# Matmul operands at multiples of 512 bytes: small tiles move out from between the pools

## The chip, the cores and the metric

One core of a Trainium2 chip. The metric is the device time of the program in microseconds, the median of several runs. "PE" is TensorE, "PEld" its weight loads, "DVE" VectorE, "ACT" ScalarE, "POOL" GpSimd, "SP" the queue that issues all DMAs here. A matmul has a stationary operand, loaded ahead of it, and a moving operand that streams through it; in `mm<-al,ch` the moving one is `al`, the stationary one `ch`, and the result goes to `mm`.

## The reference

A two-layer decoder trunk on one sequence of 1024 tokens and 1024 channels, in float32:

```python
for l in range(DEPTH):                      # two layers
    hn = rms_norm(h, norm_mix_pre[l])
    if l < N_A_LAYERS:                      # layer A: RG-LRU with a causal conv and a GELU gate
        proj = hn @ w_in_a[a]
        ...
        y = rg_lru(xr, ...) * jax.nn.gelu(gate)
    else:                                   # layer B: sliding-window attention with sinks
        proj = hn @ w_in_b[b]
        ...
        y = sliding_window_attention_with_sinks(q, shared_k, shared_v, sinks[b])
    m_out = memory_attention(mq, mk, mv)    # 4 heads over 256 memory rows
    mixed = jnp.concatenate([y, m_out], axis=-1) @ w_out[l]
    h = h + rms_norm(mixed, norm_mix_post[l])
    f = swiglu_ffn(rms_norm(h, norm_ffn_pre[l]), w_ffn_in[l], w_ffn_out[l])   # 1024 -> 2816 -> 1024
    h = h + rms_norm(f, norm_ffn_post[l])
    if l == N_A_LAYERS - 1:                 # keys and values of all B layers, made once
        kv = rms_norm(h, norm_kv) @ w_kv_shared
```

## The kernel before

Everything is held transposed: channels in partitions, tokens along them, in tiles of 128 x 512 (two halves of the sequence). Each float32 operand is split into a high part, cast to the matmul's reduced type (`ah`, `wh`, `th`, `ch`), and a low part, the difference (`al`, `wl`, `tl`, `cl`). A product is three matmuls, high weight with low data, high with high, low with high, added up in one PSUM tile. Nearly all matmuls are of this kind, with 128 x 128 weights and 512 columns: L163 to L165 in the mixers' projections, L699 to L701 in the FFN's gate and up products (`gated`, with `al`/`ah` or `tl`/`th` as the data and `ch`/`cl` as weights), L807 to L809 in the FFN's output products (`out_step`). Both FFN matrix products are written as seven half-size products each instead of eight. Casts of weights run on ACT (L94), the subtractions for the low parts on DVE (L95).

The program runs in phases: a (layer A's mixer), f0 (its FFN, with the turn to layer B at the end), b (layer B's mixer), f1 (its FFN). A scheduler sets the order of instructions; manual dependencies (`after`, `place`, `pin`) hold the products in a given order. `finish` in `mix_out` adds the residual at the start of a phase f: its loads (L109, here into `th`/`tl`) feed DVE's L630.

Where a tile lies in its partition comes from the pools. Five pools stand for the whole program: `consts` (`cp`), `act` (`ap`, `ah` and `al`), `acc` (`fp`), `stat` (`sp`) and one in DRAM. Each phase then opens its own pools behind them, in the order in which `phase` gets them, and `reuse_waits="tile"` lets a tile of the next phase wait for just the tiles that lay in its place. A pool's start is rounded up to 32 bytes and no further, so a small tile in one pool shifts the start of all that follow. With 16 KB reserved and some constants, `cst` (560 bytes) starts at 16512, `ident` (the identity for transposes) behind it at 17088; `halo`, `carry`, `nm`, `sm`, `es`, `xr` (515 columns) stand between or ahead of larger tiles.

Where the operands of the 9,207 matmuls start, in bytes above a multiple of 512 (from the built program's addresses; 7,516 matmuls have 512 columns, 1,064 have 256):

| operand | before | after |
|---|---|---|
| moving | 480: 4,680; 160: 3,444; 192: 483; 96, 224, 288 or 416: 600 | 0: 8,724; 128: 385; 192: 98 |
| stationary | 160: 7,550; 224: 676; 480: 460; 416: 416; others: 105 | 0: 9,130; others: 77 |

Before, 480 is `ah` and `al`, 160 are `th`, `tl`, `ch`, `cl`, `wh`, `wl`, 192 is `ident` (385) and `ones` (98). All those of 512 columns start at an odd multiple of 32 bytes. After, 128 is `ident`, 192 `ones`, and the 77 are columns of `rc` and `ident`.

Of the kernel before, what the change touches and what calls it, by code (L numbers as in the profile page):

```python
# [7 lines left out]
F32 = mybir.dt.float32  # L8
# [5 lines left out]
P = 128  # L14
# [7 lines left out]
NL = 6  # L22
# [28 lines left out]
class Trunk:  # L51
# [190 lines left out]
    def rcol(self, s, tag, w=H):  # L242
        nc = self.nc
        nb = w // P
        st = self.psum("oo")
        s = s if isinstance(s, list) else [s]
        cells = [(j, x) for x in s for j in range(nb)]
        self.marks.append([nc.tensor.matmul(st[:, j:j + 1], x[:, j * P:(j + 1) * P], self.ones,  # L248
                                            start=i == 0, stop=i == len(cells) - 1)
                           for i, (j, x) in enumerate(cells)])  # L250
        rc = self.tile(self.sp, 1, f"rc{tag}", (P, nb), F32)
        self.mean = nc.vector.tensor_scalar(rc, st[:, :nb], 1.0 / D, EPS, op0=ALU.mult, op1=ALU.add)
        self.pow = nc.gpsimd.tensor_tensor(rc, rc, self.mhalf[:, :nb], op=ALU.pow)
        return rc
# [19 lines left out]

    def constants(self):
        nc, cp = self.nc, self.cp
        self.cst = cp.tile([P, NC_COLS], F32, name="cst")
        with self.tc.high_priority(offset=2 * WEIGHT_LEAD):
            nc.sync.dma_start(self.cst, self.a["cst"])
        self.ident = cp.tile([P, P], F32, name="ident")  # L280
        make_identity(nc, self.ident)
        self.ones = cp.tile([P, 1], F32, name="ones")
        nc.gpsimd.memset(self.ones, 1.0)
        self.mhalf = cp.tile([P, 4], F32, name="mhalf")
        nc.gpsimd.memset(self.mhalf, -0.5)

    def lambda_const(self, prev):
        nc, cp = self.nc, self.cp
        lam = self.cst[:, C_LAM:C_LAM + NL]
        t = [cp.tile([P, NL], F32, name=f"lam{i}") for i in range(5)]  # L290
        e, d, s, s2, h = t
        nc.scalar.activation(e, lam, AF.Abs)
        self.table(e, e, AF.Exp, scale=-1.0)
        self.after(nc.vector.tensor_scalar(d, e, 2.0, None, op0=ALU.add), prev)
        nc.vector.reciprocal(d, d)
        nc.vector.tensor_tensor(s, e, d, op=ALU.mult)
        nc.vector.tensor_tensor(s2, s, s, op=ALU.mult)
        self.after(nc.vector.memset(h, 1.0 / 19.0), prev)
        for q in (17, 15, 13, 11, 9, 7, 5, 3, 1):
            nc.vector.tensor_tensor(h, h, s2, op=ALU.mult)  # L300
            nc.vector.tensor_scalar(h, h, 1.0 / q, None, op0=ALU.add)
        nc.vector.tensor_tensor(h, h, s, op=ALU.mult)
        self.after(nc.vector.tensor_scalar(d, lam, 0.0, None, op0=ALU.min), prev)
        self.cl = cp.tile([P, NL], F32, name="cl")
        self.cl2 = cp.tile([P, NL], F32, name="cl2")
        nc.vector.scalar_tensor_tensor(self.cl, h, -2.0, d, op0=ALU.mult, op1=ALU.add)
        nc.vector.tensor_scalar(self.cl2, self.cl, 16.0, None, op0=ALU.mult)
        nc.vector.tensor_scalar(self.cl, self.cl, 8.0, None, op0=ALU.mult)
# [336 lines left out]
    def quad(self, x):  # L645
        return x.rearrange("p (k c) -> p k c", k=4)
# [358 lines left out]
    def run(self):  # L1005
        a = self.a
        self.constants()
        self.h1 = self.dp.tile([D, T], F32, name="h1")
        self.kv1 = [self.dp.tile([P, H], F32, name=f"mkv1_{i}") for i in range(2)]
        common = dict(s=2, sq=1, rsn=2)  # L1010
        att = dict(qs=2, pb=4, ph=2, pl=2, nm=6, sm=6, es=6)
        mix_w = dict(wraw=2, wh=2, wl=2)
        quad = lambda i: {f"t{h}{i}{k}": 1 for h in "hl" for k in range(4)}
        ffn = ({"mm": 7, "oo": 1}, dict(ch=4, cl=4), dict(c1=2, c6=1, c7=1, hd=7, x=1),
               dict(wq=6, wp=4), quad(2), quad(3), quad(1))
        self.phase("a", {"gt": 2, "mm": 3, "ss": 1, "tt": 1, "oo": 1}, mix_w, {**common, "sp": 1}, dict(rest=1),
                   dict(xr=4, graw=1, gwh=2, gwl=2, xc=2, xh=1, xl=1, gr=2, gi=2, a2=2), att)
        spare = [("xr", (P, 3 + H)), ("gr",), ("gi",), ("a2",)]
        mix = self.mix_out(0, *self.layer_a(), a["xT"], (), spare)
        self.phase("f0", *ffn)  # L1020
        h0, fin = self.ffn(0, *mix, self.h1, False)
        self.phase("b", {"mm": 3, "ss": 2, "tt": 2, "oo": 1}, dict(wh=3, wl=3), common, dict(rest=1), dict(r=1, kf=1),
                   {**att, "qs": 4, "pb": 6})
        mix = self.layer_b(h0, fin)
        self.phase("f1", *ffn)
        self.ffn(1, *mix, a["out"], True)
        self.stack.close()
# [343 lines left out]
```

## Time and profile before

| what | us |
|---|---|
| median of 3 runs (lowest, highest) | 1978.69 (1977.61, 1980.29) |
| the profiled execution, first to last instruction | 1975.6 |
| PE busy | 1948.1 (99%) |
| DVE busy | 1398.9 (71%) |
| ACT busy | 1015.4 (51%) |
| POOL busy | 420.9 (21%) |

The profiled execution's own time is not listed apart from its span; the runs lie 2.0 to 4.7 us above that span. A matmul's duration in the trace (some 390 ns) overlaps the next ones', so its cost is the distance from its start to the next start. A row of stages gives the stretch, its length, then for each engine its busy time and number of instructions, the granted clock of PE, the mean busy share of the DMA engines and GB/s. A row of the timeline gives start, duration, engine, line, operation and tiles; a row of groups ends in the group's busy time, the mean duration of one in ns, and the idle time before them.

### The profile page before, as it was taken

The page shows a single profiled execution, that of the slowest core. Times are in us where ns is not written, and L with a number is a line of the kernel's source. Part 1 is how long each engine was busy: PE and PEld are TensorE (multiplying, and loading weights), DVE is VectorE, ACT ScalarE, POOL GpSimd, SP SyncE. Part 2 cuts the span into 40 slices and gives each one's busy share as a digit, 9 for nine tenths or more (in the row PEclk, how much of TensorE's full clock was granted, in tenths as well). Part 3 has the DMA queues.
Part 4 walks back from the last instruction along what each step waited for, and adds up shares of the span by engine and source line. Part 5 has one row for each costly group of instructions (what it writes and reads, how often), then busy time and mean ns, then how long its engine had stood idle before and what let it go on. Part 6 is the DMA issues. An engine that isn't in the chain of part 4 may idle for free.

```text
span 1975.6 us, 27850 instructions
## 1 busy us (share of the span) xinstructions
PE 1948.1 (99%) x9382; PEld 1625.9 (82%) x9382; DVE 1398.9 (71%) x2319; ACT 1015.4 (51%) x1939; POOL 420.9 (21%) x435
## 2 busy tenths in 40 slices
PE   9999999999999999999999999999999999999997
PEld 7887888788888888888788888887888888888887
DVE  8888977976766676455786898669656665754567
ACT  6677974534444444454554778454333333344551
POOL 0122200034453320000035454100223232300001
PEclk9999999999999999999999999999999999999999
DMA  5522536167768789775663423361634544586663
GB/s 184 170 85 81 162 124 226 60 231 248 246 233 278 253 283 325 234 230 176 200 213 139 126 100 111 114 251 38 207 134 165 168 146 150 200 300 192 217 193 128
DMA packets 184686, 361.71 MB, mean 183 GB/s; under 512 B 20448, under 2 KB 26336, under 8 KB 184544
## 3 DMA queue, kind: packets, MB, share of 16 engines
q1 hardware_dynamic: 184544, 359.95, 54.4%
q8 instruction: 73, 1.20, 0.2%
q14 instruction: 69, 0.57, 0.1%
HBM read 251.86 MB, written 105.91 MB: 181 GB/s over the span
## 4 chain that ended last, share of the span: by engine, by line
PE 89%; DVE 6%; issue 2%; ACT 2%; DMA 2%; POOL 0%; SPq 0%; POOLq 0%; DVEq 0%; ACTq 0%
PE mm L699 12%; PE mm L701 12%; PE mm L700 12%; PE mm L807 7%; PE mm L808 7%; PE mm L809 7%; PE mm L163 7%; PE mm L165 7%; PE mm L164 7%; PE oo L1186 1%; PE tt L1179 1%; PE mm L679 1%; PE mm L678 1%; PE mm L680 1%; PE oo L248 1%
## 5 line engine op out<-in xcount | busy, mean ns | idle before, releaser
L94 ACT CAST ch<-wq 128x512 fp32r<-128x512 f32 x311 | 193.1, 621 | 426.9 <-PE mm L700 219.6
L95 DVE TENSOR_TENSOR cl<-wq,ch 128x512 fp32r<-128x512 f32 x311 | 233.6, 752 | 190.2 <-ACT ch L94 114.8
L699 PE MATMUL mm<-al,ch 128*128 128x512 f32 x640 | 252.8, 395 | 2.8 <-ACT c L729 2.8
L701 PE MATMUL mm<-ah,cl 128*128 128x512 f32 x640 | 250.9, 392 | 0.0
L700 PE MATMUL mm<-ah,ch 128*128 128x512 f32 x640 | 250.1, 391 | 0.0
L163 PE MATMUL mm<-al,wh 128*128 128x512 f32 x552 | 219.0, 397 | 0.5 <-ACT wh L94 0.5
L165 PE MATMUL mm<-ah,wl 128*128 128x512 f32 x552 | 217.9, 395 | 0.8 <-DVE wl L95 0.7
L164 PE MATMUL mm<-ah,wh 128*128 128x512 f32 x552 | 217.7, 394 | 0.0
L807 PE MATMUL mm<-tl,ch 128*128 128x512 f32 x532 | 207.5, 390 | 0.6 <-ACT ah L909 0.3
L808 PE MATMUL mm<-th,ch 128*128 128x512 f32 x532 | 207.0, 389 | 0.0
L809 PE MATMUL mm<-th,cl 128*128 128x512 f32 x532 | 206.4, 389 | 0.0
L699 PE MATMUL mm<-tl,ch 128*128 128x512 f32 x480 | 189.1, 394 | 0.0
L701 PE MATMUL mm<-th,cl 128*128 128x512 f32 x480 | 188.5, 393 | 0.1
L700 PE MATMUL mm<-th,ch 128*128 128x512 f32 x480 | 187.4, 390 | 0.0
L710 DVE TENSOR_TENSOR c<-c,mm 128x512 f32<-128x512 f32 x120 | 82.3, 686 | 107.2 <-PE mm L701 106.9
L699 PEld LDWEIGHTS mm<-al,ch 128*128 128x128 f32 x640 | 120.2, 188 | 29.5 <-ACT c L729 3.7
L701 PEld LDWEIGHTS mm<-ah,cl 128*128 128x128 f32 x640 | 120.1, 188 | 28.2
L700 PEld LDWEIGHTS mm<-ah,ch 128*128 128x128 f32 x640 | 120.2, 188 | 26.3
L165 PEld LDWEIGHTS mm<-ah,wl 128*128 128x128 f32 x552 | 103.8, 188 | 24.0 <-DVE wl L95 1.9
L163 PEld LDWEIGHTS mm<-al,wh 128*128 128x128 f32 x552 | 103.8, 188 | 21.4 <-ACT wh L94 0.9
L164 PEld LDWEIGHTS mm<-ah,wh 128*128 128x128 f32 x552 | 104.0, 188 | 21.0
L719 POOL TENSOR_TENSOR x<-wq,wq 128x512 f32<-128x512 f32 x36 | 49.5, 1375 | 328.5 <-DMA wq<-in_wi_dram 278.6
(415 smaller groups left out, 4310.4 us busy)
## 6 DMA issues: line engine op xcount, KB each, us to landing
wq<-in_wi_dram SPq DMA_DIRECT2D x168, 256.0 KB, 4.7
xz<-hd SPq DMA_DIRECT2D x154, 256.0 KB, 4.2
th<-xz SPq DMA_DIRECT2D x154, 256.0 KB, 3.6
wp<-in_wf_dram SPq DMA_DIRECT2D x112, 256.0 KB, 4.2
wz<-wp SPq DMA_DIRECT2D x88, 256.0 KB, 2.3
wq<-wz SPq DMA_DIRECT2D x56, 256.0 KB, 3.5
wraw<-in_wa_dram SPq DMA_DIRECT2D x26, 512.0 KB, 3.5
wq<-in_wf_dram SPq DMA_DIRECT2D x42, 256.0 KB, 3.8
```

The costliest lines, as they stand in the source:

```text
L94: self.cast = self.nc.scalar.copy(hi, src)
L95: return (eng or self.nc.vector).tensor_tensor(lo, src, hi.bitcast(F32), op=ALU.subtract)
L163: self.mms += [nc.tensor.matmul(out, wh, al, start=i == 0, stop=False), nc.tensor.matmul(out, wh, ah, start=False, stop=False), nc.tensor. ...
L164: nc.tensor.matmul(out, wh, ah, start=False, stop=False),
L165: nc.tensor.matmul(out, wl, ah, start=False, stop=i == len(ks) - 1)]
L699: ins += [mm(out, wh, xl, start=start and k == 0, stop=False, skip_group_check=not start), mm(out, wh, xh, start=False, stop=False, skip_g ...
L700: mm(out, wh, xh, start=False, stop=False, skip_group_check=not start),
L701: mm(out, wl, xh, start=False, stop=k == 3, skip_group_check=not start)]
L710: add = lambda o, x, y: nc.vector.tensor_tensor(o, x, y, op=ALU.add)
L807: ins += [mm(ps[m], wh[:, m], xl[:, cs], start=start and p == 0, stop=False, skip_group_check=not start), mm(ps[m], wh[:, m], xh[:, cs], s ...
L808: mm(ps[m], wh[:, m], xh[:, cs], start=False, stop=False, skip_group_check=not start),
L809: mm(ps[m], wl[:, m], xh[:, cs], start=False, stop=p == NFB // 2 - 1, skip_group_check=not start)]
```

## The change

Tiles that no matmul reads, or that are small, move away from between the matmul operands. `ident` goes ahead of `cst`. The small columns `rc` go from the pool `stat` to the constants, which fill up to a multiple of 512. The temporaries `lam0` to `lam4`, `xr`, `halo`, `carry`, `nm`, `sm`, `es` and `nsink` go to a last pool of phase a or b.

```diff
-        rc = self.tile(self.sp, 1, f"rc{tag}", (P, nb), F32)
+        rc = self.tile(self.cp, 1, f"rc{tag}", (P, nb), F32)
...
+        self.ident = cp.tile([P, P], F32, name="ident")
         self.cst = cp.tile([P, NC_COLS], F32, name="cst")
...
-        self.ident = cp.tile([P, P], F32, name="ident")
         make_identity(nc, self.ident)
...
-        t = [cp.tile([P, NL], F32, name=f"lam{i}") for i in range(5)]
+        t = [self.t(f"lam{i}", (P, NL)) for i in range(5)]
...
-        att = dict(qs=2, pb=4, ph=2, pl=2, nm=6, sm=6, es=6)
+        att, small = dict(qs=2, pb=4, ph=2, pl=2), dict(nm=6, sm=6, es=6)
...
         self.phase("a", {"gt": 2, "mm": 3, "ss": 1, "tt": 1, "oo": 1}, mix_w, {**common, "sp": 1}, dict(rest=1),
-                   dict(xr=4, graw=1, gwh=2, gwl=2, xc=2, xh=1, xl=1, gr=2, gi=2, a2=2), att)
+                   dict(graw=1, gwh=2, gwl=2, xc=2, xh=1, xl=1, gr=2, gi=2, a2=2), att,
+                   {**small, "xr": 4, "halo": 1, "carry": 1, **{f"lam{i}": 1 for i in range(5)}})
...
-                   {**att, "qs": 4, "pb": 6})
+                   {**att, "qs": 4, "pb": 6}, {**small, "nsink": 1})
```

The orders of PE and POOL hold the same instructions in the same order. On the other engines rows differ at one place, the turn from phase a to f0. There SP issues, before the change, the last of the residual loads (`tl`) and then the loads of FFN weights (`wq`):

```order
L109 DMA tl_726_3541<-in_xT_dram 128x512
L109 DMA tl_727_3548<-in_xT_dram 128x512
L109 DMA tl_728_3555<-in_xT_dram 128x512
L109 DMA tl_729_3562<-in_xT_dram 128x512
L653 DMA wq_3396<-in_wi_dram 128x512
L653 DMA wq_3398<-in_wi_dram 128x512
L653 DMA wq_3623<-in_wi_dram 128x512
L653 DMA wq_3625<-in_wi_dram 128x512
```

and with the change:

```order
L109 DMA tl_731_3545<-in_xT_dram 128x512
L109 DMA tl_732_3552<-in_xT_dram 128x512
L653 DMA wq_3400<-in_wi_dram 128x512
L109 DMA tl_733_3559<-in_xT_dram 128x512
L653 DMA wq_3402<-in_wi_dram 128x512
L653 DMA wq_3627<-in_wi_dram 128x512
L653 DMA wq_3629<-in_wi_dram 128x512
L653 DMA wq_3631<-in_wi_dram 128x512
L109 DMA tl_734_3566<-in_xT_dram 128x512
```

The third and fourth `tl` moved behind one and four loads of weights; they now lie where phase a's `qs` tiles lay, and wait for PE's last reads of those. At the same place ACT casts, before,

```order
L94 CAST th32_701_3368<-wq_711_3396 128x512
L94 CAST th33_703_3370<-wq_712_3398 128x512
L94 CAST ah_657_3151<-acc_602_2859 128x512
L94 CAST ah_659_3156<-acc_612_2903 128x512
L223 ACTIVATE sq_679_3267<-acc_678_3265 128x512
```

and with the change:

```order
L94 CAST th32_706_3372<-wq_716_3400 128x512
L94 CAST ah_662_3154<-acc_607_2862 128x512
L94 CAST th33_708_3374<-wq_717_3402 128x512
L94 CAST ah_664_3159<-acc_617_2906 128x512
L223 ACTIVATE sq_684_3270<-acc_683_3268 128x512
```

One cast of an FFN weight (`th33`) and one of the second half's activations (`ah`) changed places; DVE's subtractions for `tl33` and `al` do the same.

## The prediction

> **What bounds the kernel now.** I read the page first (busy times, then the chain that ended last), then the granted clock, then the busy times by stage, and then single matmuls in the timeline.
>
> ```profile
> span 1975.6 us, 27850 instructions
> ...
> PE 1948.1 (99%) x9382; PEld 1625.9 (82%) x9382; DVE 1398.9 (71%) x2319; ACT 1015.4 (51%) x1939; POOL 420.9 (21%) x435
> ...
> PE 89%; DVE 6%; issue 2%; ACT 2%; DMA 2%; POOL 0%; SPq 0%; POOLq 0%; DVEq 0%; ACTq 0%
> ```
>
> TensorE is busy for 99% of the span and carries 89% of the chain. Its idle time is 1975.6 - 1948.1 = 27.5 us. The clock is no issue:
>
> ```profile
> core 0: 1975.6 us, clock 0.997
> ```
>
> The stages (layer a's mixer, FFN 0 with its end, the turn to layer b, layer b, FFN 1, the tail), with PE, PEld, DVE, ACT, POOL, clock and DMA share:
>
> ```profile
> 0.00:400.00 400.00, 391.50 (x1911) 325.92 (x1912) 327.92 (x524) 274.25 (x470) 52.01 (x91) 1.00 0.41 136
> 400.00:950.00 550.00, 549.66 (x2411) 450.73 (x2410) 361.99 (x523) 247.81 (x438) 135.08 (x96) 1.00 0.74 249
> 950.00:1000.00 50.00, 49.19 (x228) 40.47 (x227) 38.75 (x69) 25.15 (x48) 4.88 (x4) 1.00 0.51 172
> 1000.00:1330.00 330.00, 325.12 (x1914) 284.69 (x1913) 257.10 (x582) 207.10 (x527) 118.74 (x167) 0.99 0.44 152
> 1330.00:1950.00 620.00, 618.12 (x2806) 509.96 (x2805) 399.77 (x586) 259.57 (x454) 108.83 (x77) 1.00 0.53 174
> 1950.00:1975.60 25.60, 14.52 (x122) 14.16 (x121) 13.34 (x37) 1.51 (x4) 1.41 (x2) 0.83 0.38 129
> ```
>
> In the two FFN stages (1170 us) TensorE has no idle time worth the name, VectorE is busy 65% of the time and the DMA engines 53 to 74%. In the mixers VectorE is at 82% and 78%. So the time is the number of matmuls times their distance, and a change that moves no instruction acts through that distance or not at all. The durations of matmuls overlap; the distance is taken from start to start. A long run in layer a (moving operands `al`, `ah`) and one in FFN 0's output product (`tl`, `th`), first and last row of each:
>
> ```profile
> 318.05 0.39 PE L165 MATMUL mm<-ah,wl 128*128 128x512 f32 x1
> ...
> 326.29 0.39 PE L165 MATMUL mm<-ah,wl 128*128 128x512 f32 x1
> ```
>
> ```profile
> 840.20 0.39 PE L807 MATMUL mm<-tl,ch 128*128 128x512 f32 x1
> ...
> 859.92 0.39 PE L807 MATMUL mm<-tl,ch 128*128 128x512 f32 x1
> ```
>
> The first holds 36 distances: 8.24 / 36 = 228.9 ns. The second holds 87: 19.72 / 87 = 226.7 ns. Same instruction, width and clock, another distance. What differs is where the moving operand starts: 480 bytes above a multiple of 512 in the first, 160 in the second (the table of starts stands with the change; the trace holds no addresses). Groups by operand, mean duration of one:
>
> ```profile
> L699 PE MATMUL mm<-al,ch 128*128 128x512 f32 x640 | 252.8, 395 | 2.8 <-ACT c L729 2.8
> L701 PE MATMUL mm<-ah,cl 128*128 128x512 f32 x640 | 250.9, 392 | 0.0
> L700 PE MATMUL mm<-ah,ch 128*128 128x512 f32 x640 | 250.1, 391 | 0.0
> ...
> L807 PE MATMUL mm<-tl,ch 128*128 128x512 f32 x532 | 207.5, 390 | 0.6 <-ACT ah L909 0.3 <-DVE tl L95 0.3
> L808 PE MATMUL mm<-th,ch 128*128 128x512 f32 x532 | 207.0, 389 | 0.0
> L809 PE MATMUL mm<-th,cl 128*128 128x512 f32 x532 | 206.4, 389 | 0.0
> L699 PE MATMUL mm<-tl,ch 128*128 128x512 f32 x480 | 189.1, 394 | 0.0
> L701 PE MATMUL mm<-th,cl 128*128 128x512 f32 x480 | 188.5, 393 | 0.1
> L700 PE MATMUL mm<-th,ch 128*128 128x512 f32 x480 | 187.4, 390 | 0.0
> ```
>
> The output product's mean of 389.3 goes with 226.7 ns, so a duration less 162.6 is a distance: 230.1 for `al`/`ah` (392.7), 229.7 for `tl`/`th` in the gate products (392.3). Weighted over the 640, 532 and 480 triples that is 229, and I use 229.1 for the 7,516 matmuls of 512 columns. What could they be? Around 1128 us the clock was halved for a moment (0.50 in the first row), and 256 columns ran there:
>
> ```profile
> 1127.70:1128.60 0.90, 0.90 (x6) 0.90 (x6) 0.87 (x5) 0.40 (x2) 0.90 (x3) 0.50 0.11 27
> ```
>
> ```profile
> 1127.71 0.41 PE L1186 MATMUL oo<-pl,vv 128*128 128x256 f32 x1
> ...
> 1128.56 0.41 PE L1179 MATMUL tt<-ident,pb 128*128 128x128 f32 x1
> ```
>
> Four distances, 0.85 / 4 = 212.5 ns at half clock, thus 106 at the full one and 213 for 512 columns. The 226.7 is 17/16 of 213.3, the 229.1 is 7.4% over it. At full clock 256 columns show the same proportion, with both kinds of start (160, then 480):
>
> ```profile
> 82.45 0.28 PE L355 MATMUL mm<-wh,al 128*128 128x256 f32 x1
> ...
> 83.36 0.28 PE L357 MATMUL mm<-wl,ah 128*128 128x256 f32 x1
> ```
>
> ```profile
> 1930.07 0.28 PE L807 MATMUL mm<-al,th 128*128 128x256 f32 x1
> ...
> 1931.01 0.28 PE L809 MATMUL mm<-ah,tl 128*128 128x256 f32 x1
> ```
>
> Eight distances each: 113.8 and 117.5 ns against 106. So the stretch grows with the columns, is absent at half clock (moving data come too slowly for the full clock, not for the half) and depends on the start. The weight load beside it is not the cause: of four matmuls before a pause the last had none beside it, and 1.07 = 3 x 0.227 + 0.39, its usual duration:
>
> ```profile
> 944.53 1.07 PE L809 MATMUL mm<-th,cl 128*128 128x512 f32 x4
> ...
> 944.54 0.64 PEld L809 LDWEIGHTS mm<-th,cl 128*128 128x128 f32 x3
> ```
>
> **The change, part by part.** *Instructions.* None is added or removed; TensorE's and GpSimd's orders are equal, and of the others a few rows swap at the turn from layer a to FFN 0. There two residual loads (`tl`) now wait until TensorE has read the `qs` tiles that lie in their place, with a weight load queued behind each on SP.
>
> ```profile
> 313.90 2.31 SPq L109 DMA_DIRECT2D tl<-in_xT_dram  x4
> 318.10 7.67 SPq L653 DMA_DIRECT2D wq<-in_wi_dram  x8
> ...
> L165 PE MATMUL mm<-ah,qs x4: 388/388/388, 303.2 to 305.3; 128*128 128x512 f32 x4
> ...
> 344.84 2.73 DVE L630 SCALAR_TENSOR_TENSOR acc<-acc,cst,tl 128x512 f32<-128x512 f32 x4
> ```
>
> `qs` is read for the last time at 305.7 (305.3 and its 0.39), 8 us ahead of these loads; VectorE wants the data at 344.8. The `wq` loads went out until 325.8 because they wait for VectorE, not for SP. I cost this at 0, covered by some 19 us; were the cover gone, a late load of some 5 us would be the price, once. The swap of one cast on ACT and one subtraction on VectorE (0.6 and 0.7 us) is 0 as well.
>
> *Small tiles.* `rc` and the lambda tiles are the same instructions at another place: 0.
>
> *Operand starts, 512 columns.* From an odd multiple of 32 bytes, 9,130 of 9,207 stationary and 8,724 moving operands go to a multiple of 512. No row shows a 512-column matmul from such a start. Bounds: 213.3 ns from below (the half-clock rows), and from above 232.5, the slowest stretch of several, in which moving and stationary operands start alike (all at 160):
>
> ```profile
> 1701.92 0.40 PE L699 MATMUL mm<-tl,ch 128*128 128x512 f32 x1
> ...
> 1702.85 0.39 PE L700 MATMUL mm<-th,ch 128*128 128x512 f32 x1
> ```
>
> (four distances, 0.93 / 4). I take 216, near the lower end, because all that the rows show of the stretch (proportion, clock, start) fits a read that begins inside a piece of the memory's own grid and has to fetch one piece more for every sixteen; on the grid this piece is gone. That is an inference, not a row. Gain: 7,516 x (229.1 - 216) = 98 us. The Trainium skill, "TensorE: Matmul & The Clock Gate", section "Back-to-back issue gap", gives N / 2.4 + 2.5, that is 216 ns for 512 columns, measured with bf16; by it this term would be the same 98 us, and the trace, with 226.7 at best, does not reach it today.
>
> *256 columns.* 1,064 matmuls, between 113.8 and 117.5 now, say 117; to 109 by the same proportion: 8.5 us.
>
> *Given back.* VectorE does the same work in less time. In 0 to 400 us it would be busy 328 of some 379 us (87% instead of 82%), in 1000 to 1330 us 257 of 313. TensorE's idle time there is 8.5 and 4.9 us; I let it double and take 10 us for both with the loads' tighter deadlines (the DMA share of 0.74 becomes 0.78). At worst the mixers gain nothing and only the 1170 us of the FFNs do: 106 x 1170 / 1976 = 63.
>
> Sum: 98 + 8.5 - 10 = 96 us off the profiled span of 1975.6, to about 1879. The median of the runs, 1978.7, lies 3.1 over that span, so 1978.7 - 96 = 1883. Own range of this case: 1866 (213.3 ns, nothing given back: 119 + 8.5 less some 15 that VectorE takes) to 1916 (63 gained).
>
> **The rivals.** *Another steady state.* The offset matters, but what is left is the 17/16, and all stretches fall to the best one seen: 7,516 x (229.1 - 226.7) = 18 and 1,064 x (117 - 113.8) = 3.4 us, thus 1957 (1950 to 1972). For it: 226.7 holds through runs of 20 us and more and looks like a lock. Against it: it takes a supply that is too slow for the full clock from any start.
>
> *Nothing.* The contents of a read are contiguous, and a start at a multiple of 32 may be as good as any; then 1979, within 4 us. The differences between 226.7 and 229 would come from the order of the tiles and stay. Against it: within one run of one kind the distance is steady, and it turns with the tile's pool. The Trainium skill, "SBUF — State Buffer", section "Specifications (TRN2)", speaks for this rival: the memory has lines of 16 bytes. Both starts are multiples of 16, so 2,048 bytes touch 128 lines before and after, and by that rule the time stays; the same rule would have no room for the two distances above.
>
> *Slower.* With all operands on one offset the moving and the stationary stream always start on the same part of the memory. If they hinder each other there, every 512-column matmul goes like the stretch at 1702 us: 7,516 x (232.5 - 229.1) = 26 us, thus 2004. For it: that stretch has equal offsets. Against it: the output products have equal offsets too, at 226.7, the best there is. It decides from a mean distance of 229.7 on (229.1 + 4 us / 7,516).
>
> **How the numbers follow.** Forecast 0.52, another steady state 0.18, nothing 0.14, slower 0.14, the rest below 1866. Within 0.2% (4 us, about what runs of this kernel tell from no change): 0.14. Faster by more: 0.52 + 0.18 + 0.02, rounded to 0.71. Slower: 0.15. The range reaches from 1866 over the forecast, the steady state and no change to 1981 and leaves out the slower case; the likeliest case alone has 1866 to 1916.
>
> **What would show it.** Right: 694 matmuls of the output product, 157 us of FFN 0 now, take about 150; group means of L699 to L701 and L807 to L809 fall alike to about 378; `al` and `tl` groups no longer differ. Idle time of TensorE grows in the mixers alone, behind VectorE. Wrong: group means at 389 everywhere (the steady state), unchanged and still apart (nothing), at 395 or over (slower). A late `tl` load would stand as a wait of L630 near 340 us. The step that I trust least is 216.

## The result, and the profile after

| | median us (lowest to highest, runs) | span of the profiled run |
|---|---|---|
| before | 1978.34 (1977.61 to 1980.29, 4) | 1975.6 |
| after | 1966.66 (1965.88 to 1969.17, 4) | 1964.7 |

The ratio is 0.9946 (95% interval 0.9931 to 0.996): faster by 0.5%, some 12 us by the medians and 11 by the spans, of the 96 that were forecast. The page after (span, busy times, chain):

```profile
span 1964.7 us, 27857 instructions
...
PE 1935.3 (99%) x9382; PEld 1626.5 (83%) x9382; DVE 1397.8 (71%) x2319; ACT 1015.5 (52%) x1939; POOL 426.0 (22%) x435
...
PE 88%; DVE 6%; ACT 2%; issue 2%; DMA 1%; POOL 1%; SPq 0%; POOLq 0%; DVEq 0%; ACTq 0%
```

TensorE's busy time fell by 12.8 us (1948.1 to 1935.3) and its idle time rose by 1.9 (27.5 to 1964.7 - 1935.3 = 29.4): 10.9 us of span. The stages that were shown of before, with PE, PEld, DVE, ACT, POOL, clock, DMA share:

```profile
0.00:400.00 400.00, 390.24 (x1915) 326.14 (x1916) 327.73 (x524) 274.61 (x471) 55.09 (x91) 1.00 0.40 136
400.00:950.00 550.00, 549.01 (x2427) 453.74 (x2427) 366.33 (x531) 250.74 (x444) 134.80 (x95) 1.00 0.73 250
...
1330.00:1950.00 620.00, 618.00 (x2874) 517.04 (x2875) 402.57 (x599) 258.50 (x453) 110.98 (x78) 1.00 0.53 176
```

The stretch from 400 to 950 us, nearly all of 512 columns, holds more matmuls (2,427 for 2,411) in the same busy time: each costs less. The last stretch (2,874 for 2,806) can't be read that way, since the program runs ahead and 78 more of its matmuls have 256 columns (250 for 172), while those of 512 fell from 2,580 to 2,556. How much less one costs is read from start-to-start distances in the timeline, for the two stretches that stood at 228.9 and 232.5 ns (the second with its block at another time now):

```profile
316.52 0.39 PE L165 MATMUL mm<-ah,wl 128*128 128x512 f32 x1
...
324.68 0.39 PE L165 MATMUL mm<-ah,wl 128*128 128x512 f32 x1
...
1691.21 0.39 PE L699 MATMUL mm<-tl,ch 128*128 128x512 f32 x1
...
1692.12 0.39 PE L700 MATMUL mm<-th,ch 128*128 128x512 f32 x1
```

36 distances in 8.16 us are 226.7 ns, four in 0.91 are some 227. In the groups, the gate products (L699 to L701) have come down to the 389 to 390 ns that the output products (L807 to L809) had before, and those have not moved. The mixers' projections (L163 to L165) have come down less, from 397, 394 and 395 to 395, 393 and 393.

```profile
L699 PE MATMUL mm<-al,ch 128*128 128x512 f32 x640 | 249.6, 390 | 2.9 <-ACT c L729 2.9
L700 PE MATMUL mm<-ah,ch 128*128 128x512 f32 x640 | 249.2, 389 | 0.0
L701 PE MATMUL mm<-ah,cl 128*128 128x512 f32 x640 | 249.0, 389 | 0.0
L163 PE MATMUL mm<-al,wh 128*128 128x512 f32 x552 | 218.2, 395 | 0.6 <-ACT wh L94 0.6
...
L807 PE MATMUL mm<-tl,ch 128*128 128x512 f32 x532 | 207.4, 390 | 0.6 <-ACT ah L909 0.3 <-DVE tl L95 0.3
L808 PE MATMUL mm<-th,ch 128*128 128x512 f32 x532 | 207.0, 389 | 0.0
L809 PE MATMUL mm<-th,cl 128*128 128x512 f32 x532 | 206.4, 389 | 0.0
L699 PE MATMUL mm<-tl,ch 128*128 128x512 f32 x480 | 187.4, 390 | 0.2
```

From the start times of all 512-column matmuls, leaving out distances over 250 ns (pauses), the mean went from 229.12 to 227.17 ns: 7,516 x 1.95 = 14.7 us. The matmuls of 256 columns became slower, from 117.2 to 119.4 ns (distances over 150 ns left out): 1,064 x 2.2 = 2.3 us the other way. 14.7 - 2.3 = 12.4 accounts for the 12.8 us of busy time.

### The profile page after: what moved, and what is told of

Read it like the earlier page. It is cut to its first block, busy times and chain, and to the rows that moved or that the text cites. A ratio compares the mean times of both kernels' runs of the same rounds, so it can differ in the third digit from the quotient of the medians.

```text
span 1964.7 us, 27857 instructions
## 1 busy us (share of the span) xinstructions
PE 1935.3 (99%) x9382; PEld 1626.5 (83%) x9382; DVE 1397.8 (71%) x2319; ACT 1015.5 (52%) x1939; POOL 426.0 (22%) x435
## 4 chain that ended last, share of the span: by engine, by line
PE 88%; DVE 6%; ACT 2%; issue 2%; DMA 1%; POOL 1%; SPq 0%; POOLq 0%; DVEq 0%; ACTq 0%
PE mm L699 12%; PE mm L701 12%; PE mm L700 12%; PE mm L807 7%; PE mm L808 7%; PE mm L809 7%; PE mm L165 6%; PE mm L163 6%; PE mm L164 6%; PE oo L1187 1%; PE tt L1180 1%; PE oo L248 1%; PE mm L679 1%; PE mm L678 1%; PE mm L680 1%
## 5 line engine op out<-in xcount | busy, mean ns | idle before, releaser
L699 PE MATMUL mm<-al,ch 128*128 128x512 f32 x640 | 249.6, 390 | 2.9 <-ACT c L729 2.9
L701 PE MATMUL mm<-ah,cl 128*128 128x512 f32 x640 | 249.0, 389 | 0.0
L163 PE MATMUL mm<-al,wh 128*128 128x512 f32 x552 | 218.2, 395 | 0.6 <-ACT wh L94 0.6
L165 PE MATMUL mm<-ah,wl 128*128 128x512 f32 x552 | 216.9, 393 | 0.9 <-DVE wl L95 0.9
L807 PE MATMUL mm<-tl,ch 128*128 128x512 f32 x532 | 207.4, 390 | 0.6 <-ACT ah L909 0.3
L808 PE MATMUL mm<-th,ch 128*128 128x512 f32 x532 | 207.0, 389 | 0.0
L809 PE MATMUL mm<-th,cl 128*128 128x512 f32 x532 | 206.4, 389 | 0.0
L699 PE MATMUL mm<-tl,ch 128*128 128x512 f32 x480 | 187.4, 390 | 0.2
L701 PE MATMUL mm<-th,cl 128*128 128x512 f32 x480 | 186.5, 389 | 0.4 <-DVE cl L95 0.4
L699 PEld LDWEIGHTS mm<-al,ch 128*128 128x128 f32 x640 | 120.2, 188 | 28.4 <-ACT c L729 3.7
L701 PEld LDWEIGHTS mm<-ah,cl 128*128 128x128 f32 x640 | 120.2, 188 | 25.0
L165 PEld LDWEIGHTS mm<-ah,wl 128*128 128x128 f32 x552 | 103.7, 188 | 23.4 <-DVE wl L95 2.1
L163 PEld LDWEIGHTS mm<-al,wh 128*128 128x128 f32 x552 | 103.8, 188 | 21.1 <-ACT wh L94 1.0
```

Of the source, the lines that this page charges most:

```text
L163: self.mms += [nc.tensor.matmul(out, wh, al, start=i == 0, stop=False), nc.tensor.matmul(out, wh, ah, start=False, stop=False), nc.tensor. ...
L165: nc.tensor.matmul(out, wl, ah, start=False, stop=i == len(ks) - 1)]
L699: ins += [mm(out, wh, xl, start=start and k == 0, stop=False, skip_group_check=not start), mm(out, wh, xh, start=False, stop=False, skip_g ...
L701: mm(out, wl, xh, start=False, stop=k == 3, skip_group_check=not start)]
L807: ins += [mm(ps[m], wh[:, m], xl[:, cs], start=start and p == 0, stop=False, skip_group_check=not start), mm(ps[m], wh[:, m], xh[:, cs], s ...
L808: mm(ps[m], wh[:, m], xh[:, cs], start=False, stop=False, skip_group_check=not start),
```

## The experiments

**Streams by themselves.** Nothing but matmuls in float32r, 48 of each kind back to back; the decoder is not computed. The moving tile starts at a chosen offset, the stationary one at another (`sta` at 0, `stb`, `stc`, `std` at 32, 160 and 480 bytes here), all else alike. Each of the three kernels of streams in this section ran once.

```python
for i, c in enumerate(ABC):                      # offa, offb, ...: 0, 32, ... 480 bytes
    stream(mov[c], 8 * i, 512, st["a"], 0)
for n in (448, 384, 320, 256, 192, 128):
    stream(mov["a"], 0, n, st["a"], 0)
...
for c, so in (("b", 8), ("c", 40), ("d", 120)):  # stationary off, moving at 0
    stream(mov["a"], 0, 512, st[c], so)
```

> A kernel of matmuls alone (the output is not the reference's): streams of 48 matmuls without any wait, each stream with another start of the moving operand (tiles offa to offp: 0, 32, 64 ... 480 bytes above a multiple of 512; 512 columns), then other widths from start 0 (448 to 128 columns), 256 columns from eight starts, three starts of the stationary operand (stb 32, stc 160, std 480), and bf16. Theory 'settled stream' (the start's value matters little, each matmul pays 13.3 ns however wide): 226.7 ns at every start, 200, 173, 147, 120 for 448 to 256 columns. Theory 'state by start': 226.7 at 0 and 160, 229 at 480. The theory of my prediction, a grid of at least 64 bytes: a start on the grid would be near 216; after the change this should show nowhere, since 0 gave 226.7. Proportional stretch of 17/16: 198, 170, 142, 113 for 448 to 256 columns. If the 4-byte moving data set the limit, bf16 runs at some 216; if it is a cost of every matmul, bf16 stays at 226.7.

The groups (mean duration of one behind the busy time; for 512 columns the distance is some 162.6 less):

```profile
L44 PE MATMUL bank<-bfm,bfs 128*128 128x512 bf16 x96 | 20.9, 379 | 0.0
L44 PE MATMUL bank<-offa,sta 128*128 128x512 f32 x48 | 13.1, 438 | 6.3 <-DVE offa L30 6.3
...
L44 PE MATMUL bank<-offb,sta 128*128 128x512 f32 x48 | 11.4, 395 | 0.0
...
L44 PE MATMUL bank<-offa,stb 128*128 128x512 f32 x48 | 11.4, 395 | 0.0
...
L44 PE MATMUL bank<-offk,sta 128*128 128x512 f32 x48 | 11.2, 392 | 0.0
L44 PE MATMUL bank<-offi,sta 128*128 128x512 f32 x48 | 11.0, 389 | 0.0
...
L44 PE MATMUL bank<-offa,sta 128*128 128x384 f32 x48 | 8.5, 334 | 0.0
...
L44 PE MATMUL bank<-offa,sta 128*128 128x256 f32 x48 | 5.9, 283 | 0.0
```

From the start times, the mean of each stream's last 36 distances, in ns:

| what | distance |
|---|---|
| moving at 256 (`offi`), stationary at 0 | 226.7 |
| moving at 0 (`offa`, the first stream; its last 30 alone stand at 226.7) | 227.0 |
| at 64 or 320 (`offc`, `offk`) | 228.9 |
| at 32, 96, 128, 192, 224 and the same + 256 | 233.3 |
| at 160 or 416 | 234.2 |
| moving at 0, stationary at 32, 160 or 480 | 233.3 |
| start 0, 384 / 320 / 256 columns | 173.3 / 146.7 / 120.0 |
| 256 columns, moving at 32 / 64 bytes | 116.7 / 117.8 |
| bf16, 512 / 256 columns | 215.8 / 109.2 |

Three things follow. The start counts, and both operands do, with a period of 256 bytes: 256 is as good as 0. Even at the best start the 226.7 stays. And what is over the columns' own time (0.4167 ns each) is 13.3 ns at 512, 384, 320 and 256 columns (16 at 448, whose 202.8 is the one exception): a fixed amount for each matmul, not a share. The columns' own time comes from the first stream, whose group (mean 438) holds a slower state: behind a first distance of 592 ns stand eight of 426.7, which is twice 213.3, or 512 x 0.4167, with nothing over. It is half the pace, though the profile lists the granted clock of that stretch as 1.00. For the starts, neither theory on record was right: there are no equal distances at all starts, and 160 and 480 (234.2, 233.3) are as slow as 32 (233.3). The fixed 13.3 ns and some 216 for bf16 were forecast.

**The changed kernel, started elsewhere.** The streams suggest that the difference between the two operands' starts decides; it was not among the theories on record for these runs. If it does, the changed kernel keeps its time when everything moves together, and loses it when moving and stationary operand part. Two kernels put a tile behind the constants, which moves all operands alike to 160 or to 480 bytes above a multiple of 512; a third puts it in `stat`, so that `ah` and `al` stay at 0 and the phases' pools (weights, `th`, `tl`) go to 160.

```diff
+        self.pad = cp.tile([P, 40], F32, name="pad")      # 160 bytes; 120 columns for 480
+        nc.gpsimd.memset(self.pad, 0.0)
```
```diff
+        self.nc.gpsimd.memset(self.sp.tile([P, 40], F32, name="pad"), 0.0)     # the third
```

> The changed kernel with 160 bytes more in the constants: all operands start 160 above a multiple of 512, all alike. 'Settled stream, one start for all': as the changed kernel, 1967 us. 'The multiple of 512 itself': the gain goes, 1978. 'State by start' (160 settles at 226.7, as the output products did before): 1967, with 256 columns perhaps at 113 to 116 instead of 120, some 4 us less.

> The changed kernel with 480 bytes more in the constants: all operands start 480 above a multiple of 512. 'One start for all': 1967 us. 'The multiple of 512 itself': 1978. 'State by start' (480 runs at 229, as al and ah did before): 7,516 x 2.3 ns = 17 us above the changed kernel, 1984.

> The changed kernel with 160 bytes in the pool stat: ah, al and acc stay at 0, the operands of the phases' pools are at 160. Both starts settle at 226.7 alone, if the trace of before is right. 'One start for all' (each switch between starts upsets the stream for some matmuls): part of the gain goes, 1970 to 1976 us. 'State by start': switches cost nothing, 1967.

| | median us (lowest to highest, 5 runs each) | ratio to before, at 1977.07 beside these (95%) | mean distance, 512 columns |
|---|---|---|---|
| all at 160 | 1966.62 (1965.63 to 1968.23) | 0.9945 (0.9932 to 0.9959) | 227.2 |
| all at 480 | 1967.54 (1967.01 to 1970.9) | 0.9953 (0.9941 to 0.9966) | 227.2 |
| 0 and 160 | 1991.52 (1990.57 to 1994.04) | 1.0075 (1.0062 to 1.0087) | 231.3 |

Groups of the gate product, all at 480, and then, with 0 and 160, of the gate product and of the output product (L808):

```profile
L701 PE MATMUL mm<-al,ch 128*128 128x512 f32 x640 | 249.6, 390 | 2.8 <-ACT c L731 2.8
```

```profile
L702 PE MATMUL mm<-ah,cl 128*128 128x512 f32 x640 | 254.3, 397 | 0.0
L700 PE MATMUL mm<-al,ch 128*128 128x512 f32 x640 | 253.6, 396 | 2.0 <-ACT c L730 2.0
...
L808 PE MATMUL mm<-tl,ch 128*128 128x512 f32 x532 | 207.5, 390 | 0.6 <-ACT ah L910 0.3 <-DVE tl L96 0.3
...
L700 PE MATMUL mm<-tl,ch 128*128 128x512 f32 x480 | 188.7, 393 | 0.0
```

The multiple of 512 is worth nothing by itself: starts at 160 or 480 are as good. With 0 and 160 the gate products of `al` and `ah` rise to 396 while the output products of `tl`, which share the weights' start, stay at 390; the gate products of `tl` rise to 393, to which the next experiment comes back. 1991.5 is outside what any theory on record gave for this run (1967 to 1976). By the built program's addresses 4,146 matmuls then differ by 96 modulo 256 from the weights of the matmul behind them, which are loaded while they stream (4,152 from their own): 4,146 x (233.3 - 226.7) = 27 us estimated. The mean distance gives more, 7,516 x (231.3 - 227.2) = 31 us, and TensorE's busy time rose by 30.7 (1935.3 to 1966.0); the rest is about what the gate products of `tl` and `th` lost (229.7 for 226.8 by their start times). Idle time fell by 3.5, so that the span is 27.2 us longer (1991.9 against 1964.7; 24.9 by the medians). That this meets the 27 is in part luck.

**The kernel before, with 64 bytes more.** The addresses also say what was amiss before: 4,092 matmuls of 512 columns had starts that differ by 64 modulo 256 from the next one's weights, and 3,372 by 0 (from their own, 4,152 and 3,316). So a tile of 64 bytes in the kernel before should bring what the whole change brought, without one operand at a multiple of 512.

```diff
+        self.nc.gpsimd.memset(self.sp.tile([P, 16], F32, name="pad"), 0.0)
```

> The kernel before, with one tile of 64 bytes more in the pool stat, so that the phases' pools start 64 bytes later: ah and al stay at 480 bytes above a multiple of 512, ch, cl, wh, wl, th and tl come to 224. No operand of 512 columns lies at a multiple of 512, or of 64; but moving and stationary operand differ by 256 or 0 for 7,418 matmuls of 512 columns. 'It is the difference modulo 256 bytes': as the changed kernel, 1965 to 1970 us, group means of L699 to L701 for al/ah at 389 to 390 ns. 'The multiple of 512' or 'one start for all, modulo 512': as before, 1975 to 1980 us, with al/ah at 392 to 395 ns. 'Any difference other than 0 costs': 1990 or more.

1967.47 us (1965.37 to 1968.59, 5 runs), ratio 0.9949 (0.9935 to 0.9963; the kernel before stood at 1977.4 beside it): the changed kernel's time, as the difference modulo 256 had it on record, while the multiple of 512 stood there with 1975 to 1980.

```profile
L700 PE MATMUL mm<-al,ch 128*128 128x512 f32 x640 | 249.6, 390 | 2.9 <-ACT c L730 2.9
...
L700 PE MATMUL mm<-tl,ch 128*128 128x512 f32 x480 | 187.5, 391 | 0.2
```

The second row bears on the gate products of `tl` and `th`, which differed by 0 before and stood at 394, 390 and 393 all the same. Here their own difference is 0 still, only the neighbouring blocks of `al` and `ah` have changed theirs, and they fall to 391, 389 and 389. Their start alone (224 for 160) is not the reason, since with all operands at 160 this group shows 390 and 389 too. So a disturbed block costs the block behind it as well, and the trace of before shows it by place: in blocks of `tl`/`th` gate products, which follow blocks of `al`/`ah`, the first ten distances average 230.8 ns, the eleventh and twelfth 226.7. With the change, or with these 64 bytes, the first ten average 226.7 and 226.8.

**What is left at the best start.** Two more kernels of streams alone. The first has narrower stationary operands, finer offsets, and two streams in which a matmul's own weights and the next one's differ in start (24 columns are 96 bytes):

```python
for c, o in zip("bcdefghi", (1, 2, 4, 12, 20, 28, 36, 60)):   # offb ... offi: 4 to 240 bytes
    stream(mov[c], o, st["a"], 0)
for c, d in (("j", 0), ("k", 1)):                # j: alike with the own weights, k: with the next
    for i in range(48):
        x = 24 * ((i + d) % 2)
        y = 24 * (i % 2)
        mm(st["b"][:, y:y + 128], mov[c][:, 0, x:x + 512], 512, 128)
for c, m in (("l", 64), ("m", 32)):              # m columns of weights
    stream(mov[c], 0, st["c"], 0, m=m)
    stream(mov[c], 24, st["d"], 0, m=m)
```

> Matmul streams only, 48 of a kind, the decoder is not computed; figures are steady distances from start to start. Two theories of the 13.3 ns that a float32r matmul takes over its columns (226.7 against 213.3 for 512). 'The weight load takes the moving stream's reads': the 13.3 ns go with the columns of the next weight load, so 512 columns beside loads of 64 columns take 220.0 and beside loads of 32 columns 216.7 at difference 0, and what the start adds (233.3 at 96 bytes) shrinks too. 'A fixed price of the type': 226.7 and 233.3 whatever the load's width. Which load counts: moving and own stationary operand alike while the next stationary lies 96 bytes off gives 233.3 if it is the next load that runs beside the stream, 226.7 if it is the own; the reverse stream gives 226.7 and 233.3. Finer starts, stationary at 0: a period of 256 bytes and lines of 16 would leave 4 and 8 bytes at 226.7 or a little over, and 16, 48, 80, 112, 144 and 240 bytes at 233.3; if 64 bytes is a bank (228.9 there before), 16 and 48 lie between 226.7 and 233.3.

Groups, first the matmuls, then the weight loads:

```profile
L37 PE MATMUL bank<-offb,sta 128*128 128x512 f32 x48 | 11.5, 399 | 0.0
L37 PE MATMUL bank<-offj,stb 128*128 128x512 f32 x48 | 11.4, 396 | 0.0
...
L37 PE MATMUL bank<-offm,stc 128*32 128x512 f32 x48 | 11.3, 394 | 0.0
...
L37 PE MATMUL bank<-offl,stc 128*64 128x512 f32 x48 | 11.2, 392 | 0.0
...
L37 PE MATMUL bank<-offk,stb 128*128 128x512 f32 x48 | 11.2, 392 | 0.0
```

```profile
L37 PEld LDWEIGHTS bank<-offe,sta 128*128 128x128 f32 x48 | 9.0, 188 | 2.0
...
L37 PEld LDWEIGHTS bank<-offl,stc 128*64 128x64 f32 x48 | 6.4, 134 | 4.6
...
L37 PEld LDWEIGHTS bank<-offm,stc 128*32 128x32 f32 x48 | 5.2, 109 | 5.9
```

Loads of 64 and 32 columns are shorter (134 and 109 ns for 188), but 512 columns beside them take 230.0 and 231.7 ns at difference 0, not 220 and 217: the width of the load does not set the 13.3 ns at this length. At 256 columns it does count (113.3 beside 64 columns of weights, 120.0 beside 128). At a difference of 96 bytes, 512 columns take 231.4 and 233.4 ns beside the narrower loads, for 233.3. Between own and next weights the answer is not clean: alike with the next 230.0, with the own 234.0, so the next counts for more, but neither stream reaches 226.7. Small offsets are no better than large: 4 bytes 236.7, 8 bytes 233.3, 16 bytes 231.7, 48 bytes 230.0, 80 and 112 bytes 231.1, 144 and 240 bytes 233.3; nothing lies under 226.7.

The second asks what kind of price it is: the moving operand with every second column read (`offe`), the stationary one likewise (`offf`), operands of 64 partitions (`offd`), a result bank other than its neighbour's for each matmul (`offg`), and the same weights each time (`offc`).

```python
mm(st["b"][:64, i // 3 % 4 * 128:i // 3 % 4 * 128 + 128], mov["d"][:64, 0, :512], 512, 128)
...
mm(st["b"][:, i // 3 % 4 * 128:i // 3 % 4 * 128 + 128], flat["e"][:, :1024:2], 512, 128)
...
mm(st["c"][:, i // 3 % 4 * 64:i // 3 % 4 * 64 + 256:2], mov["f"][:, 0, :512], 512, 128)
```

> Matmul streams only, 48 of a kind, float32r, the decoder is not computed; steady distances from start to start, all operands at difference 0. What are the 13.3 ns over 213.3 that 512 columns keep at the best start? 'The memory's supply' (what the predicted 216 ns rested on, a read that has to fetch pieces): with every second column read (8 bytes from column to column, twice the range) the moving stream needs twice the pieces, so well over 226.7, 240 or more; with operands of 64 partitions the same 226.7 if each partition has its own port, less if the sum counts. 'A fixed price of the instruction': 226.7 with every second column, with 64 partitions, with the same 128 weights each time, and with each matmul its own group in another bank. 'The accumulation into one bank': 215.8 with a bank for each matmul. 'The weight load's reads': more with every second weight column read, 226.7 with the moving operand spread. And on the start: moving operand fixed, the stationary one alternating between 0 and 96 bytes gives some 230 (half 226.7, half 233.3), alternating between 0 and 256 bytes 226.7.

```profile
L39 PE MATMUL bank<-offe,stb 128*128 128x512 f32 x48 | 21.9, 634 | 0.0
L39 PE MATMUL bank<-offf,stc 128*128 128x512 f32 x48 | 11.4, 394 | 0.0
...
L39 PE MATMUL bank<-offd,stb 64*128 64x512 f32 x48 | 11.2, 389 | 0.0
...
L39 PE MATMUL bank<-offg,sta 128*128 128x512 f32 x48 | 11.0, 389 | 0.0
```

Every second column read doubles the distance: 451.1 ns for the same 512 columns. This fits a stream that is bound by the range of memory that it goes over, at 4 bytes in 0.4167 ns: dense float32r would then need all of that rate at full clock and have nothing to spare, while bf16 with half the bytes loses 2.5 ns (215.8), and at half the pace (426.7) nothing is lost. It isn't proof: steps other than one and two were not tried, so a price for any step but one is not excluded. A fixed price of the instruction alone would have left `offe` at 226.7; and what `offe` keeps over twice the columns' time (451.1 - 426.7 = 24.4) is itself nearly twice 13.3, so the 13.3, fixed over the widths, does not stay fixed here. Neither 64 partitions, nor a bank of its own, nor the same weights each time change the 226.7, so it is neither a total over the partitions nor the accumulation. Weights with every second column read bring 233.3, 6.7 ns more: how the load reads matters to the stream, if not its width. A stationary operand that alternates between 0 and 96 bytes gave 230.0, half of each, and between 0 and 256 bytes 226.7, as the difference modulo 256 has it.

What a matmul loses the fixed 13.3 ns to is not settled. Streams without any weight load beside them were not tried: here each matmul brings its own load. No run showed a layout faster than the changed kernel's.

## Why the prediction was wrong, point by point

- *What bounds it.* Right: the time goes by the matmuls' distance. It fell by 1.95 ns for 7,516 matmuls, and the time with it.
- *Instructions; the moved `tl` loads at 0.* Right. The third and fourth went out at 317.7 and 320.1 us, and VectorE went from `th` to `tl` without a pause:

```profile
317.74 0.38 SPq L109 DMA_DIRECT2D tl<-in_xT_dram  x1
318.21 1.84 SPq L653 DMA_DIRECT2D wq<-in_wi_dram  x4
320.14 0.38 SPq L109 DMA_DIRECT2D tl<-in_xT_dram  x1
...
341.24 2.73 DVE L630 SCALAR_TENSOR_TENSOR acc<-acc,cst,th 128x512 f32<-128x512 f32 x4
343.89 2.73 DVE L630 SCALAR_TENSOR_TENSOR acc<-acc,cst,tl 128x512 f32<-128x512 f32 x4
```

- *Operand starts, 512 columns: the step that failed.* "I take 216 [...] on the grid this piece is gone": at a multiple of 512 the distance is 226.7, the best that the trace of before had shown already. Three links broke. The "17/16" is no proportion: 13.3 ns are lost at 256, 320, 384 and 512 columns alike. The second width that the prediction took for it was read too kindly: 113.8 and 117.5 against 106 are 7% and 11%, and by the table of starts those two stretches (moving `wh` at 160 with `al` at 480, moving `al` at 480 with `th` at 160) differ by 192 and 64 modulo 256, so neither could be set beside the 226.7 at difference 0. That the stretch "is absent at half clock" was read as a supply too slow for the full clock, and every second column read, at twice the distance, fits that; but it gave no licence to call the whole loss a matter of the start. And "The weight load beside it is not the cause" rested on the modelled end of one last matmul: the runs show that the start of the stationary operand alone moves the distance from 226.7 to 233.3. What makes up the 13.3 ns that stay stays open.
- *The bounds.* 213.3 from below was no row of a start, only the columns' own time; the nearest row at full clock was 226.7, and by it the term was 18 us. Measured: 14.7 instead of 98. Before, 4,092 matmuls at difference 64 made 4,092 x (228.9 - 226.7) = 9 us of this; the gate products of `tl` and `th`, disturbed by their neighbours, 1,440 x (229.7 - 226.7) = 4 more, an estimate from the prediction's 229.7 (their start times give 230.0 before and 226.8 after, 4.7 us). The upper bound of 232.5 was such a place: its four distances are the first of a `tl`/`th` block, right behind one of `al`/`ah`:

```profile
1701.69 0.39 PE L701 MATMUL mm<-ah,cl 128*128 128x512 f32 x1
1701.92 0.40 PE L699 MATMUL mm<-tl,ch 128*128 128x512 f32 x1
```

- *256 columns, 8.5 us.* Wrong in sign: 117.2 became 119.4. At this width difference 0 is not the best (120.0; 32 bytes 116.7, 64 bytes 117.8). 80 us into the program eight distances that took 0.91 us take 0.96:

```profile
82.46 0.28 PE L355 MATMUL mm<-wh,al 128*128 128x256 f32 x1
...
83.42 0.28 PE L357 MATMUL mm<-wl,ah 128*128 128x256 f32 x1
```

- *Given back, 10 us.* Not put to the test, since little was gained: 1.9 us of idle time more.
- *The rivals.* "Another steady state" is what happened in kind: the stretches fall to the best one seen, and 1966.66 lies in its 1950 to 1972. Its 1957 was some 10 us too low, by the 256 columns (3.4 us off expected, 2.3 on found), by what the mean keeps over 226.7 (18 us expected, 14.7 found), and by idle time (1.9). "Slower", by equal offsets that hinder each other, is refuted: at 512 columns equal offsets are the best case, and the stretch that spoke for it was slow from the block ahead. "Nothing" had the Trainium skill, "SBUF — State Buffer", section "Specifications (TRN2)", for it: lines of 16 bytes, and at least two hits in each for the full rate. Multiples of 16 bytes did differ (226.7 to 234.2), and with two hits in each line `offe` took 451.1 against 226.7, so for this stream the measurement decides against both readings. The formula of the Trainium skill, "TensorE: Matmul & The Clock Gate", section "Back-to-back issue gap", N / 2.4 + 2.5, holds for bf16 here (215.8 and 109.2); for float32r at full clock it does not (226.7), and the forecast's 216 is what it gives. Its cold form, N / 1.2, is met by the eight float32r distances of 426.7.

## What to carry to other kernels

Read the distance from start to start, not the duration: where identical matmuls show two distances, compare the two operands' starts, and for float32r matmuls of 512 columns let moving and stationary tile differ by a multiple of 256 bytes (at 256 columns 32 or 64 bytes were better); 64 bytes in one pool did here what a change of all pools did. A multiple of 512 is not needed. The smallest distance that a trace already shows for the same form is the forecast of what an alignment can bring, until a stream by itself has shown a smaller one; and a loss seen at one width is a share only when a second width, at the same difference of starts, says so.

## What the runs showed of the hardware

- A float32r matmul of 512 columns takes 226.7, 228.9, 233.3 or 234.2 ns, depending on (moving start - stationary start) modulo 256 bytes, at multiples of 32; bf16 takes 215.8 at both starts tried (0 and 32 bytes).
- A float32r matmul of 512 columns at a step of 8 bytes takes 451.1 ns, for 226.7 at a step of 4; that the range of memory sets this is an inference.
- A stream of matmuls with an unfavourable difference also slows the next one: the first ten distances of a block at difference 0 behind one at 64 average 230.8 ns, then 226.7.
- After a change of streams the distance needs some matmuls to settle (236, 228, 233, 230, then 227 where weights alternating between 0 and 256 bytes follow weights alternating between 0 and 96), so a mean over short blocks lies over the steady one.
- At 192 and 128 columns the distance stays at 111.7 ns, with loads of 128 float32r columns, for 120.0 at 256 columns: below that a narrower matmul gains little.
